# Layer norm at the end of a transformer layer: earlier broadcast, sums on GpSimd, and the last tokens normalised out of PSUM in another order

## The chip, the cores and the metric

The kernel runs on one core of one Trainium2 chip. A core has five engines with a queue each: TensorE (PE: matrix products, written into PSUM), VectorE (DVE), ScalarE (ACT), GpSimd (POOL) and SyncE (SP, which here issues the transfers). The metric is the device time of one execution in microseconds; lower is better. A kernel's time is the median of its runs.

## The reference, cut to what matters

One layer of a diffusion transformer on 1024 tokens of width 1024 (all float32): attention, a layer norm, a SwiGLU feed-forward block with a convolution along the tokens, and a second layer norm. Only the last two lines are touched by the change:

```python
y = _conv_ffn(h, w_up, conv_w, conv_b, w_down)          # silu(gate) * val, then @ w_down
x = _layer_norm(DEEPNORM_ALPHA * x + gate2 * y, ln2_g, ln2_b)

def _layer_norm(x, g, b):
    mu = mean(x); var = mean((x - mu) ** 2)
    return (x - mu) * rsqrt(var + LN_EPS) * g + b
```

## The kernel before

Activations lie transposed: 128 channels of one of eight channel blocks f on the partitions, tokens along the row. Each float32 operand of a product is split into two parts, hi (`hd`, a cast on ScalarE, line 82) and lo (`ld`, a subtraction on VectorE, line 87), and a product of a pair is three matmuls (lines 90 to 92).

The down projection at the end is built from seven products over half the tokens each, p = 1, 6, 2, 7, 4, 5 in a loop, and a seventh, 3, after it. One product has 11 steps k; a step multiplies four channel blocks f with 512 tokens, so four groups of three matmuls. The pair of step k is loaded, cast and split about three steps ahead (`dnext`, `dload`), into rings of four slots, so that the pair of step 10 gets its slot when step 6 has been multiplied. A finished product is added from PSUM into the residual `zz` by VectorE (`accum`, line 1437); these evictions are issued within the next product.

After product 4 the first 512 tokens (`h0`) are complete, and their layer norm runs beside product 5: `ln_steps` (line 1018) makes a list of steps: statistics (tiny matmuls against a column of ones, then a few small operations and a power on GpSimd), diagonals (line 978), the broadcast of 1/sigma and of mean/sigma over the partitions (matmuls at line 1048, copied out by ScalarE at line 1050), and then for each f an apply: a product on VectorE (line 1055), a subtraction (line 1057, with LN2_P = 1 always on GpSimd), and the output with weight and bias on ScalarE (line 1430) with its transfer. Each step carries a gap. `tick` adds columns / 0.8 to a counter after every group of three matmuls and issues the next step when the counter has reached its gap. LN2_D holds the gaps for the first half: before the statistics, the diagonals, the broadcast, the first apply, and each further apply. The steps are queued in step k = 3 of product 5 and the counter starts from zero there.

After product 5 come the casts and splits of the last four pairs of product 3, product 5's evictions (four of its own sums with `modc`, four with `nmod`), then the third quarter (tokens 512 to 767; product 3, tiles `yl`, 256 columns): the first seven steps for all four f, then for each f the last four steps, an `accum`, the sums for the layer norm (`ln_add`: `zs` the sum, line 998, and `zq` the sum of squares, line 999, the squares by ScalarE at line 997), and `tok`, which transposes the block of the last 256 tokens into PSUM tiles `zt` (line 1560). The tiles `zt` of the first call take the banks that product 5's first two blocks have held. The third quarter's layer norm (LN2_E) runs beside the last quarter's product.

The last quarter (two blocks t of 128 tokens) is normalised with tokens on the partitions: `zt[a][t]` holds one half a of the channels, mean and variance come from the batch-norm statistics (lines 1563 and 1597), `bmv` holds mean and then 1/sigma, and four tiles `ot[t, a]` are made, weighted, biased and sent (lines 1602 to 1620).

The order of TensorE's queue is that of the program (the manual schedule opened at line 1177). The queues of the other engines are ordered by the language's planner, which takes the program's order as priority and its own idea of when an instruction is ready; on the chip each queue then runs strictly in that order and waits at each instruction for what it needs.

Of the kernel before, what the change touches and what calls it, by code (L numbers as in the profile page):

```python
# [7 lines left out]
F32 = mybir.dt.float32  # L8
R32 = mybir.dt.float32r
AF = mybir.ActivationFunctionType  # L10
ALU = mybir.AluOpType
AX = mybir.AxisListType

P = 128
# [21 lines left out]
SPAN = 0.8, 0.85  # L36
LN1_F = 3500.0, 5100.0, 100.0
LN1_D = (2500.0, 2000.0, 2000.0, 2500.0), (300.0, 3700.0, 300.0, 500.0), (100.0, 1000.0, 300.0, 500.0)
LN2_D = 5000.0, 4000.0, 2500.0, 1500.0, 700.0
LN2_E = 3500.0, 3000.0, 1500.0, 800.0, 500.0  # L40
NCL = 3
BLD = 2400.0
# [6 lines left out]
D3AT = (7, 5), (7, 9), (4, 1), (4, 4), (4, 7), (4, 10), (5, 2)  # L49
NXS = 5  # L50
RAWB = 3
OTP = (0, 0), (1, 0)
OTO = (0, 0), (0, 1), (1, 0), (1, 1)
OTK = 4
OTA = 1
# [14 lines left out]
def layer_kernel(  # L70
# [6 lines left out]
    nc = tc.nc  # L77
# [55 lines left out]
    def ht(name, shape=(P, T), dt=F32):  # L133
        hslot[name] = pool, tag = hfree.pop(0)
        return pool.tile(list(shape), dt, tag=tag, name=name, bufs=1)
# [94 lines left out]
    for k in range(KT):  # L230
# [5 lines left out]
        for t in range(NT):  # L236
            s = slice(t * P, (t + 1) * P)
# [463 lines left out]
    for n, (gi, k) in enumerate(order):  # L701
# [9 lines left out]
        nm, src, tiles = groups[gi]  # L711
# [4 lines left out]
        for t in tiles:  # L716
            if t < NT:
                s = slice(t * P, (t + 1) * P)
                a = hT[k][0][:, s], hT[k][1][:, s]
            else:  # L720
                s = slice((t - NT) * P, (t - NT + 1) * P)
                a = c[0][:, s], c[1][:, s]
# [164 lines left out]
    def sml(name, w=512):  # L887
        return ps3.tile([P, w], F32, tag="sml", name=name, bufs=2)
# [28 lines left out]
    def zv(f, s):  # L917
        hf = s.start // HALF
        return zt_[f % 4, hf][:, f // 4, s.start - hf * HALF:s.stop - hf * HALF]
# [24 lines left out]
    for f in range(2, KT):  # L944
# [4 lines left out]
        for j in range(4):  # L949
            k = (f % 2) * 4 + j  # L950
            for hf in (0, 1):
                a = O[1, hf, 0, j // 2][:, j % 2], O[1, hf, 1, j // 2][:, j % 2]
# [9 lines left out]
    post = tc.alloc_tile_pool(name="post", bufs=1, side="left", reuse_waits="tile")  # L962
# [26 lines left out]
    def ln_add(zf, zs, zq, s, first, nm, qe, se):  # L989
        w = s.stop - s.start  # L990
        ln_flush()
        if first:
            nc.scalar.activation(zq[:, s], zf, AF.Square)
            nc.gpsimd.tensor_scalar(out=zs[:, s], in0=zf, scalar1=1.0, scalar2=0.0, op0=ALU.mult, op1=ALU.add)
            return
        q = tm(f"sq{nm}", w=w)
        nc.scalar.activation(q, zf, AF.Square)
        se.tensor_tensor(out=zs[:, s], in0=zs[:, s], in1=zf, op=ALU.add)
        sqs.append(lambda: qe.tensor_tensor(out=zq[:, s], in0=zq[:, s], in1=q, op=ALU.add))
# [13 lines left out]
    def drain(keep=0):  # L1013
        while len(pend) > keep:
            pend.pop(0)[1]()
            clock[0] = 0.0
# [170 lines left out]
    for f in (4, 6):  # L1187
        for si in (1, 2):
# [3 lines left out]
            elif f == 6:  # L1192
                second = ln1(2)
                a = [n for n in range(len(pend)) if len(pend) - n <= KT]
# [294 lines left out]
    lnr = ht("lnr", (P, 2, HALF)), ht("lnr2", (P, 2, HALF))  # L1489
# [8 lines left out]

    def sums(f, s, first):
        ln_add(zv(f, s), zs2, zq2, s, first, f"b{f}_{s.start}", nc.vector,  # L1500
               nc.vector if s.start else nc.gpsimd)

    for p in (1, 6, 2, 7, 4, 5):
        if p == 6:
# [10 lines left out]
        def ev(f, o, p=p):  # L1515
            if p == 1:
                nc.scalar.copy(u2[f], o)
            elif p == 6:
                accum(f, h0, u2[f], False)
                nc.vector.tensor_tensor(out=u2[f], in0=u2[f], in1=o, op=ALU.subtract)  # L1520
            elif p == 2:
                accum(f, h0, o, True)
                sums(f, h0, f == 0)
                accum_affine(f, h1, u2[f], True)
            elif p == 7:
                nc.vector.tensor_tensor(out=u3[f], in0=u2[f], in1=o, op=ALU.add)
                accum(f + 4, h0, u3[f], True)
                accum_affine(f + 4, h1, u3[f], False)
                if f == 3:
                    hput("u20", "u21", "u30", "u31")  # L1530
            elif p == 4:
                accum(f + 4, h0, o, True)
                sums(f + 4, h0, False)
            else:
                accum(f + 4, h1, o, False)
                sums(f + 4, LN2_S[1], f == 0)

        evict += [lambda f=f, o=acc[f]: ev(f, o) for f in range(4)]
        if p == 4:
            after.append(lambda: pend.extend(ln_steps(zs2, zq2, h0, "b0", emit2, *LN2_D, LN2_P[0])))  # L1540
    banks[:] = sides[nside[0] % 2] + sides[nside[0] % 2 ^ 1]
# [6 lines left out]
    s = LN2_S[-1]  # L1548
    w = s.stop - s.start
    nt = w // P  # L1550
    zt = {}
    bst = post.tile([P, nt, 2, 6], F32, tag="bst", name="bst")
    mv = post.tile([P, nt, 2], F32, tag="bmv", name="bmv")
    nm = post.tile([P, nt], F32, tag="bnm", name="bnm")

    def tok(f):
        if f % 4 == 0:
# [28 lines left out]
    for f in range(4):  # L1586
        o = sml(f"yl{f}_{r.start}")[:, 0:r.stop - r.start]
# [9 lines left out]
        nc.vector.bn_aggr(out=mv[:, t], in_=bst[:, t].rearrange("p a b -> p (a b)"))  # L1597
    nc.vector.tensor_scalar(out=mv[:, :, 1], in0=mv[:, :, 1], scalar1=LN_EPS, scalar2=None, op0=ALU.add)
    nc.gpsimd.tensor_tensor(out=mv[:, :, 1], in0=mv[:, :, 1], in1=mhalf[:, 0:nt], op=ALU.pow)
    nc.vector.scalar_tensor_tensor(out=nm, in0=mv[:, :, 0], scalar=-1.0, in1=mv[:, :, 1], op0=ALU.mult, op1=ALU.mult)  # L1600
    ot = {}

    def last(t, a):
        o = ot[t, a]
        nc.vector.tensor_tensor(out=o, in0=o, in1=lnr[0][:, a], op=ALU.mult)
        e = nc.gpsimd if (t, a) in OTP else nc.vector
        e.tensor_tensor(out=o, in0=o, in1=lnr[1][:, a], op=ALU.add)
        ts = slice(s.start + t * P, s.start + (t + 1) * P)
        nc.sync.dma_start(out[4 * a:4 * a + 4, :, ts].rearrange("f p q -> p f q"),
                          o.rearrange("p (f q) -> p f q", q=P))  # L1610

    drain(OTK)
    for n in OTO:
        t, a = n
        o = ot[n] = ht(f"ot{t}_{a}", (P, HALF))
        nc.scalar.activation(o, zt[a][t], AF.Identity, bias=nm[:, t:t + 1], scale=mv[:, t, 1:2])
        drain(max(len(pend) - OTA, 0))
    for t, a in OTO:
        last(t, a)
        drain(max(len(pend) - OTB, 0))  # L1620
# [116 lines left out]
```

## Time and profile before

| | |
|---|---|
| median of 3 runs | 1587.97 us (1587.14 to 1588.69) |
| span of the profiled execution, first to last instruction | 1585.4 us |
| around the span, median less span | 2.57 us |
| granted TensorE clock, mean | 0.992 |
| instructions | 22064 |

The profiled execution's own time is known by its span alone; all instants below are microseconds from the span's start. A row of a timeline has the start, the time the instruction (or the merged run, with its count) took, the engine, the line, the operation, what it writes and reads, the shapes, and in brackets the idle time of the engine before it with what ended that. A row of a table of stretches has the busy time of each engine in the stretch, the granted TensorE clock (1.00 is full speed), the share of the DMA engines and the rate. Consecutive instructions of one engine overlap by up to 0.1 us, so that a run of equal ones is shorter than their number times the time of one.

### The profile page before, as it was taken

Reading aid. Unit: us, or ns where it says so; the run is one execution under the profiler, and the core shown is the slowest. Engines: PE = TensorE matmul, PEld = TensorE weight load, DVE = VectorE, ACT = ScalarE, POOL = GpSimd, SP = SyncE. Lnnn points to the kernel's source line nnn. Section 1 sums busy time; section 2 is a strip of 40 time slices with the busy share of each in tenths; the row PEclk is TensorE's granted clock in tenths of the full one; section 3 lists DMA queues with packets and bytes.
Section 4 is the critical chain, followed back from the end, with each engine's and each line's share of the span. In section 5 each row is a group of like instructions: output and inputs, shape, how many; then the busy total and the mean of one; then the engine's idle time right before and its main releaser. Section 6 shows DMA issues by size and latency. Waiting matters only on the chain.

```text
span 1585.4 us, 22064 instructions
## 1 busy us (share of the span) xinstructions
PE 1528.4 (96%) x7680; PEld 1269.8 (80%) x7680; DVE 1195.6 (75%) x1766; ACT 813.0 (51%) x1443; POOL 753.7 (48%) x731
## 2 busy tenths in 40 slices
PE   6999999999999999999999999999999999999996
PEld 5878788878887887777788898888888888888876
DVE  7797646628888777888674779888888877657886
ACT  5422222448887667688531565444444444435642
POOL 0574302426667556665422554666667764021132
PEclk9999999999999999999999999999999999999998
DMA  9695662322236555531451132333334446996721
GB/s 378 217 313 188 221 217 81 120 80 67 62 104 157 139 127 145 118 73 39 142 186 53 60 101 86 114 107 112 115 106 118 111 113 189 358 273 210 255 94 53
DMA packets 112367, 229.98 MB, mean 145 GB/s; under 512 B 12960, under 2 KB 27808, under 8 KB 112160
## 3 DMA queue, kind: packets, MB, share of 16 engines
q1 hardware_dynamic: 96816, 198.93, 37.6%
q0 software_dynamic: 10400, 20.19, 8.2%
q10 hardware_dynamic: 5040, 9.46, 1.6%
q8 instruction: 60, 0.98, 0.3%
q14 instruction: 51, 0.42, 0.1%
HBM read 177.35 MB, written 65.86 MB: 153 GB/s over the span
## 4 chain that ended last, share of the span: by engine, by line
PE 82%; DVE 6%; ACT 4%; issue 3%; POOL 2%; DMA 2%; ACTq 0%; SPq 0%; DVEq 0%; POOLq 0%
PE ptr L531 5%; PE p L90 4%; PE p L91 4%; PE p L92 4%; PE g L90 3%; PE g L91 3%; PE g L92 3%; PE b L92 3%; PE b L91 3%; PE b L90 3%; PE s L414 2%; PE a L92 2%; PE c L91 2%; PE d L91 2%; PE c L92 2%
## 5 line engine op out<-in xcount | busy, mean ns | idle before, releaser
L541 DVE TENSOR_TENSOR ptl<-ptr,pth 128x512 fp32r<-128x512 f32 x188 | 124.8, 685 | 27.5 <-ACT pth L540 25.2
L531 PE MATMUL ptr<-ident,p 128*128 128x128 f32 x816 | 126.5, 278 | 10.3 <-DVE ptl L541 7.8
L540 ACT CAST pth<-ptr 128x512 fp32r<-128x512 f32 x188 | 106.6, 588 | 56.3 <-PE ptr L531 32.7
L87 DVE TENSOR_TENSOR ld<-rd,hd 128x1024 fp32r<-128x1024 f32 x77 | 94.0, 1240 | 52.5 <-ACT hd L82 50.4
L426 ACT ACTIVATE p<-p,nm 128x1024 f32<-128x1024 f32 (+2 forms) x128 | 125.3, 981 | 10.9 <-DVE p L459 10.1
L531 PEld LDWEIGHTS ptr<-ident,p 128*128 128x128 f32 x816 | 93.8, 140 | 40.3 <-DVE ptl L541 13.5
L82 ACT CAST hd<-rd 128x1024 fp32r<-128x1024 f32 x77 | 79.2, 1050 | 81.5 <-PE p L92 50.0
L552 PE MATMUL av<-pth,VT 128*128 128x512 f32 x236 | 104.6, 443 | 1.0 <-ACT avs L558 0.5
L90 PE MATMUL p<-hd 128*128 128x512 f32 x264 | 103.2, 391 | 0.0
L92 PE MATMUL p<-hd,ld 128*128 128x512 f32 x264 | 102.7, 389 | 0.0
L91 PE MATMUL p<-ld,hd 128*128 128x512 f32 x264 | 102.7, 389 | 0.0
L90 PE MATMUL g<-hh,whg 128*128 128x512 f32 x256 | 99.9, 390 | 0.0
L92 PE MATMUL g<-hh,wlg 128*128 128x512 f32 x256 | 99.7, 389 | 0.0
L91 PE MATMUL g<-hl,whg 128*128 128x512 f32 x256 | 99.6, 389 | 0.0
L553 PE MATMUL av<-ptl,VT 128*128 128x512 f32 x236 | 97.6, 414 | 2.0 <-POOL ptl L87 1.9
L87 POOL TENSOR_TENSOR wlg<-wg,whg 128x512 fp32r<-128x512 f32 x32 | 47.0, 1479 | 109.6 <-ACT whg L82 107.3
L459 DVE TENSOR_SCALAR_CACHE_REDUCE p<-s,cvt,nmc 128x1024 f32<-128x1024 f32 x64 | 84.5, 1340 | 12.3 <-PE s L415 11.8
L414 PE MATMUL s<-KL,q 128*128 128x512 f32 (+2 forms) x192 | 76.0, 396 | 2.9 <-ACT p_x L426 2.0
L188 DVE CUSTOM_DVE_ANT_0 wml<-wml,sc,bmc 128x1024 f32<-128x1024 f32 x32 | 45.0, 1416 | 39.0 <-DMA wml<-in_wmodT_dram 38.6
L84 POOL TENSOR_SCALAR pth<-prw 128x512 fp32r<-128x512 f32 x48 | 31.1, 649 | 88.2 <-ACT prw L537 62.7
L82 ACT CAST wS<-s 128x512 fp32r<-128x512 f32 x76 | 45.3, 621 | 52.1 <-POOL s L1079 51.3
L415 PE MATMUL s<-KL,q 128*128 128x512 f32 (+2 forms) x192 | 71.7, 373 | 0.0
(396 smaller groups left out, 4974.0 us busy)
## 6 DMA issues: line engine op xcount, KB each, us to landing
wml<-in_wmodT_dram SPq DMA_DIRECT2D x48, 512.0 KB
ru<-in_w_up_dram SPq DMA_DIRECT2D x38, 512.0 KB
rd<-td SPq DMA_DIRECT2D x55, 256.0 KB
rd<-sd SPq DMA_DIRECT2D x44, 256.0 KB
rd<-in_w_dn_dram SPq DMA_DIRECT2D x33, 256.0 KB
wm<-in_wmodT_dram SPq DMA_DIRECT2D x16, 512.0 KB
wg<-in_w_g_dram SPq DMA_DIRECT2D x32, 256.0 KB
sgd<-sg ACTq DMA_DIRECT2D x32, 256.0 KB
```

The lines of the kernel that those rows point to most:

```text
L82: nc.scalar.copy(hi, src)
L87: lo_eng.tensor_tensor(out=lo, in0=src, in1=hi.bitcast(F32), op=ALU.subtract)
L90: nc.tensor.matmul(ps, a[0], b[0], start=start, stop=False, skip_group_check=resumed)
L91: nc.tensor.matmul(ps, a[0], b[1], start=False, stop=False, skip_group_check=resumed)
L92: nc.tensor.matmul(ps, a[1], b[0], start=False, stop=stop, skip_group_check=resumed)
L414: nc.tensor.matmul(o, self.q[0][:, hs], ks, start=True, stop=False)
L426: nc.scalar.activation(p, s, AF.Exp, bias=nm[:, h:h + 1], scale=scale, accum_out=sm[:, h:h + 1])
L531: nc.tensor.transpose(tr[:, h * P:(h + 1) * P], self.pslice(h, n), ident)
L540: nc.scalar.copy(hi, tr)
L541: nc.vector.tensor_tensor(out=lo, in0=tr, in1=hi.bitcast(F32), op=ALU.subtract)
L552: nc.tensor.matmul(self.av, v, hi, start=first, stop=False)
L553: nc.tensor.matmul(self.av, v, lo, start=False, stop=self.left == 0)
```

## The change

Three edits, all at the end of the kernel:

- LN2_D, the gaps of the first half's layer norm, is changed: shorter gaps before the statistics, the diagonals, the broadcast and the first apply, a longer one between applies.
- The `zs` sums of the third quarter are issued on GpSimd in place of VectorE; the first half's were there already.
- The last tokens: before, ScalarE made (z - mean) / sigma out of PSUM, with the product -mean/sigma (`bnm`) computed ahead of it, VectorE multiplied with the weight, and VectorE or GpSimd (OTP) added the bias. Now VectorE makes (z - mean) * weight out of PSUM in one pass for all four tiles; for the first token block ScalarE then scales with 1/sigma and GpSimd adds the bias, and for the second one VectorE does both in one pass.

```diff
-LN2_D = 5000.0, 4000.0, 2500.0, 1500.0, 700.0
+LN2_D = 4000.0, 2800.0, 2000.0, 1200.0, 1300.0
...
-OTP = (0, 0), (1, 0)
+OTP = (0, 0), (0, 1)
...
     def sums(f, s, first):
         ln_add(zv(f, s), zs2, zq2, s, first, f"b{f}_{s.start}", nc.vector,
-               nc.vector if s.start else nc.gpsimd)
+               nc.gpsimd)
...
-    nm = post.tile([P, nt], F32, tag="bnm", name="bnm")
...
-    nc.vector.scalar_tensor_tensor(out=nm, in0=mv[:, :, 0], scalar=-1.0, in1=mv[:, :, 1], op0=ALU.mult, op1=ALU.mult)
...
     def last(t, a):
         o = ot[t, a]
-        nc.vector.tensor_tensor(out=o, in0=o, in1=lnr[0][:, a], op=ALU.mult)
-        e = nc.gpsimd if (t, a) in OTP else nc.vector
-        e.tensor_tensor(out=o, in0=o, in1=lnr[1][:, a], op=ALU.add)
+        if (t, a) in OTP:
+            nc.scalar.activation(o, o, AF.Identity, scale=mv[:, t, 1:2])
+            nc.gpsimd.tensor_tensor(out=o, in0=o, in1=lnr[1][:, a], op=ALU.add)
+        else:
+            nc.vector.scalar_tensor_tensor(out=o, in0=o, scalar=mv[:, t, 1:2], in1=lnr[1][:, a],
+                                           op0=ALU.mult, op1=ALU.add)
...
         o = ot[n] = ht(f"ot{t}_{a}", (P, HALF))
-        nc.scalar.activation(o, zt[a][t], AF.Identity, bias=nm[:, t:t + 1], scale=mv[:, t, 1:2])
+        nc.vector.scalar_tensor_tensor(out=o, in0=zt[a][t], scalar=mv[:, t, 0:1], in1=lnr[0][:, a],
+                                       op0=ALU.subtract, op1=ALU.mult)
```

## The prediction

> **What bounds the kernel now.** I read the page first, then the stalls of TensorE, then the stretch around its one long stall, then the end. TensorE is the bound nearly everywhere:
>
> ```profile
> PE 1528.4 (96%) x7680; PEld 1269.8 (80%) x7680; DVE 1195.6 (75%) x1766; ACT 813.0 (51%) x1443; POOL 753.7 (48%) x731
> ```
>
> The diff touches only what is issued from 1509 us on, so the waits of TensorE from 1505 us to the end come next. There is one group:
>
> ```profile
> PE zt L1560 <- DVE zz L1437: 4.1, 3, 3.4
> ```
>
> In TensorE's order of time the stall stands between the last matmul of the first column block of the third quarter and the transposes of the last tokens (start, duration, engine, line, tiles, idle before and what ended it):
>
> ```profile
> 1541.75 0.28 PE L92 MATMUL yl<-hd,ld 128*128 128x256 f32 x1
> 1545.47 0.33 PE L1560 MATMUL zt<-ident,zz 128*128 128x128 f32 x1 [3.44 <-DVE zz L1437]
> ...
> 1550.90 0.38 PE L1560 MATMUL zt<-ident,zz 128*128 128x128 f32 x2
> ...
> 1552.55 0.38 PE L1560 MATMUL zt<-ident,zz 128*128 128x128 f32 x2
> ```
>
> Without the stall the first transposes would start at 1541.87 (the matmuls are 0.12 apart) and, at the warm step of 1552.55 - 1550.90 = 1.65 per block, the fourth pair at 1541.87 + 3 x 1.65 = 1546.82. It starts at 1552.55, so this place holds 5.73 us. Part of that is the clock. The busy time and clock of single stretches (busy us of PE, PEld, DVE, ACT, POOL, then PEclk, DMA share, GB/s):
>
> ```profile
> 98.10:100.60 2.50, 0.10 (x2) 0.08 (x1) 2.50 (x4) 1.19 (x2) 2.50 (x2) 0.77 0.71 227
> 716.90:718.60 1.70, 0.14 (x2) 0.12 (x2) 1.67 (x6) 1.11 (x5) 0.47 (x2) 1.00 0.87 217
> 719.00:724.00 5.00, 5.00 (x29) 3.75 (x28) 3.86 (x7) 4.71 (x13) 0.88 (x2) 1.00 0.00 0
> 1542.00:1545.40 3.40, 0.03 (x1) 0.00 (x0) 3.40 (x9) 1.05 (x3) 0.00 (x0) 1.00 0.00 0
> 1546.80:1550.10 3.30, 3.30 (x18) 3.30 (x17) 3.06 (x8) 0.83 (x2) 0.00 (x0) 0.50 0.00 0
> ```
>
> After the stall the granted clock is 0.50 for 3.3 us, which costs half of it, 1.65. A gap of about 2.4 us near 98 us also halves the clock; one of about 1.56 us near 717 us does not, then or after. So a stall left under some 1.6 us should cost only itself.
>
> What the transposes wait for is older than the diff's last part: they are written into the PSUM banks of product 5, whose accumulations into zz VectorE finishes late. VectorE's order:
>
> ```profile
> 1518.99 1.23 DVE L87 TENSOR_TENSOR ld<-rd,hd 128x1024 fp32r<-128x1024 f32 x1 [1.35 <-ACT hd L82]
> 1520.75 11.49 DVE L1055 TENSOR_TENSOR zz<-zz,rbb 128x512 f32<-128x512 f32 x8 [0.54 <-ACT rbb L1050]
> 1532.17 0.74 DVE L1437 SCALAR_TENSOR_TENSOR zz<-p,modc,zz 128x512 f32<-128x512 f32 x1
> 1536.47 4.63 DVE L87 TENSOR_TENSOR ld<-rd,hd 128x1024 fp32r<-128x1024 f32 x4 [3.56 <-ACT hd L82]
> 1541.02 1.40 DVE L1437 SCALAR_TENSOR_TENSOR zz<-p,modc,zz 128x512 f32<-128x512 f32 x2
> 1542.34 0.41 DVE L998 TENSOR_TENSOR zs<-zs,zz 128x256 f32<-128x256 f32 x1
> 1542.67 0.42 DVE L999 TENSOR_TENSOR zq<-zq,sqb 128x256 f32<-128x256 f32 x1
> ...
> 1544.67 2.72 DVE L1437 SCALAR_TENSOR_TENSOR zz<-p,nmod,zz 128x512 f32<-128x512 f32 x4
> ```
>
> It stands idle 3.56 us for ScalarE's casts of the last four down-weight pairs, and those stand behind ScalarE's eight outputs of the first half, which follow GpSimd's eight subtractions one by one:
>
> ```profile
> 1534.69 0.81 ACT L1430 ACTIVATE of<-zz,ln2c 128x512 f32<-128x512 f32 x1 [0.44 <-POOL zz L1057]
> 1535.41 3.89 ACT L82 CAST hd<-rd 128x1024 fp32r<-128x1024 f32 x4
> ```
>
> ```profile
> 1521.66 12.99 POOL L1057 TENSOR_TENSOR zz<-zz,mbb 128x512 f32<-128x512 f32 x8 [7.68 <-ACT mbb L1050]
> ```
>
> So the chain that ends in the stall begins with the broadcast matmuls of the layer norm, a step whose place LN2_D sets: bcrb, 13 us on GpSimd, four casts, four splits, the accumulations.
>
> **The change part by part.**
>
> *Gaps (LN2_D).* The counter grows by 640 after each group of three matmuls of product 5 and the steps are queued at k = 3. Stepping it by hand gives, before: statistics after group 8, diagonals 15, broadcast 18, applies 21 to 28; after: 7, 11, 14 and 16, 18, ... 30. The broadcast moves up by four groups of three matmuls. The step of the matmuls, the two broadcasts, and the second diagonal on VectorE:
>
> ```profile
> 1518.16 0.39 PE L92 MATMUL p<-hd,ld 128*128 128x512 f32 x1
> 1518.39 0.39 PE L90 MATMUL p<-hd 128*128 128x512 f32 x1
> ...
> 1519.08 1.02 PE L1048 MATMUL bcrb<-dgrb,onesf 128*128 128x512 f32 x2
> 1519.93 1.02 PE L1048 MATMUL bcmb<-dgmb,onesf 128*128 128x512 f32 x2
> ...
> 1515.83 0.68 DVE L978 TENSOR_TENSOR dgmb<-ident,mrb 128x512 f32<-128x512 f32 x1
> ```
>
> 12 x 0.227 = 2.72 us earlier, at 1516.36. TensorE does the same work, only in another order: after the broadcasts (0.85 each by their starts) come 14 groups of 0.68, so product 5 still ends at 1519.08 + 1.7 + 9.5 = 1530.3. The diagonals have time: the second ends at 1516.5 today, and would serve a second broadcast at 1517.2 even if it did not move with the statistics. What is lost: the split of product 5's last pair (the row at 1518.99) now falls among the applies. Its ring slot is freed when TensorE's step k = 6 ends, two groups before the broadcast of before (1517.7), and the broadcasts' 1.7 us now lie inside that step (1519.4). TensorE needs that split four groups before the end of product 5, at 1527.6, so the split has 8 us for a cast of 1 and its own 1.2 to 2.3. But the applies are limited by VectorE and GpSimd excluding each other:
>
> ```profile
> L1055 DVE TENSOR_TENSOR zz<-zz,rbb x8: 687/1776/1781, 1520.8 to 1530.5; 128x512 f32<-128x512 f32 x8
> ...
> 1499.80 2.31 DVE L87 TENSOR_TENSOR ld<-rd,hd 128x1024 fp32r<-128x1024 f32 x1
> ...
> 1497.18 3.85 POOL L998 TENSOR_TENSOR zs<-zs,zz 128x512 f32<-128x512 f32 x2 [48.17 <-DVE zz L1437]
> 1498.09 0.74 DVE L1437 SCALAR_TENSOR_TENSOR zz<-p,nmod,zz 128x512 f32<-128x512 f32 x1
> ```
>
> An apply takes 0.69 alone and 1.78 beside a subtraction, a split 2.31 in place of 1.23; an accumulation with one operand in PSUM keeps its 0.74. So the split adds its own step, 4.63 / 4 = 1.16, to the chain of 13 us. The eight outputs, and with them the four casts and splits, come 2.72 - 1.16 = 1.56 earlier. Ends: 2.7 if the split slips in free, 0.9 if the first accumulation is now put behind the splits (0.66 more on the path). The new "each" of 1300 does nothing by itself: the chain's 1.7 per apply is slower than two groups of matmuls, 1.36.
>
> *Sums of the third quarter on GpSimd.* Seven zs adds leave VectorE; three of them stand ahead of the accumulation that TensorE waits for, at 0.33 each (1542.34 to 1542.67): 1.0 us off the path. On GpSimd, idle there, one takes about
>
> ```profile
> 1564.80 0.79 POOL L1057 TENSOR_TENSOR zz<-zz,mbb 128x256 f32<-128x256 f32 x1 [5.75 <-DVE zz L1055]
> ```
>
> 0.8 us, at most one every 0.7 us ahead of the stall, and the queue empties before the statistics matmuls, which LN2_E puts eleven groups of 3 x 0.12 us, 4 us, after the last block. Against it: two zq adds stay on VectorE in the same stretch, both operands in SBUF, and can be held up by a GpSimd add, as the applies are, by up to 0.5 each. Gain 0.0 to 1.0; I take 0.6, nearer to the upper end since only part of a 0.79 add excludes.
>
> [...]
>
> *Sum at the stall.* 1.56 + 0.6 = 2.2 us earlier, so TensorE idles about 1.3 of 3.44 us. That is under 1.6, so the slow clock goes too: 2.2 + 1.65 = 3.8. Ends: 0.9 (0.9 + 0.0, clock still halved) and 5.73 (stall gone). From there to 1571 us TensorE has no other wait, so the gain is carried to the tail whole. Next late would be the same accumulation, or the statistics of the third quarter: the last block's accumulation, zs add (0.8) and zq add (0.4) have those 4 us.
>
> *The tail.* Rows of before:
>
> ```profile
> 1573.44 0.17 DVE L1598 TENSOR_SCALAR bmv<-bmv 128x2 f32<-128x2 f32 x1
> 1573.69 0.70 POOL L1599 TENSOR_TENSOR bmv<-bmv,mhalf 128x2 f32<-128x2 f32 x1 [3.46 <-DVE bmv L1598]
> 1574.76 2.78 ACT L1616 ACTIVATE ot<-zt,bnm,bmv 128x512 f32<-128x512 f32 x4 [3.39 <-DVE bnm L1600]
> 1576.39 1.66 POOL L1607 TENSOR_TENSOR ot<-ot,lnr 128x512 f32<-128x512 f32 x1 [2.00 <-DVE ot L1605]
> 1579.12 1.74 DVE L1605 TENSOR_TENSOR ot<-ot,lnr 128x512 f32<-128x512 f32 x1
> ...
> 1580.34 0.94 SPq L1609 DMA_DIRECT2D out_dram<-ot  x2
> ...
> 1581.62 0.37 SPq L1609 DMA_DIRECT2D out_dram<-ot  x1
> ...
> 1581.30:1584.00 2.70, 0.00 (x0) 0.00 (x0) 0.29 (x1) 0.00 (x0) 0.00 (x0) 0.50 1.03 284
> ```
>
> Removed: the product bnm (0.16, on the path), four ScalarE passes, four VectorE products, two VectorE adds. Added: four VectorE passes out of PSUM, which need the mean alone and so start at 1573.6 beside GpSimd's power (2.72 for four, the row at 1544.67: to 1576.4); two ScalarE scalings (0.81 each, as the output at 1534.69, from 1574.5), two GpSimd adds behind them (1.66 each: 1575.3 to 1577.0 to 1578.6), and two VectorE passes for the last token block, both operands in SBUF, beside those adds (up to 1.74 each: 1576.4 to about 1579.5). The last output is issued at about 1579.5 in place of 1581.62: 2.1 us. But the outputs queue: the last three (256 KB each, the first issued at 1580.34) fill 2.7 us at 284 GB/s. If the second add's output is issued ahead of the last two, these three start from 1578.65 in place of 1580.34, 1.7; if the order lets one go earlier, up to 2.5. Ends 1.6 and 2.5; I take 2.0, the middle.
>
> *Sum.* 3.8 + 2.0 = 5.8 us off the profiled 1585.4, so a span of 1579.6. The median of the runs is 2.57 above this span, which I take for what lies around it: 1587.97 - 5.8 = 1582.2.
>
> **The rivals.**
>
> (a) *Only the tail gains.* The planner orders ScalarE and VectorE anew, and the four casts or the accumulations come as late as now; the stall stays. For it: the casts could run from 1522 on, and the planner put them behind all eight outputs. Against it: those outputs come earlier in any order. 1587.97 - 2.0 = 1586.0.
>
> (b) *The stall closes.* If the planner fills VectorE's 3.56 us of idle time with accumulations: 5.7 + 2.0 = 7.7, 1580.3.
>
> (c) *The stall shrinks, the clock still falls*, because the remaining gap is 2 us or more: 1.2 + 2.0 = 3.2, about 1584.8. [...]
>
> (d) *Slower: TensorE starves in product 5.* The first three outputs of the half are now issued ahead of product 5's last pair. If ScalarE's queue has that pair's cast behind them, it waits for GpSimd, 1.70 per output. The last output ends at 1535.5 today and so at 1532.8, the one of place j (0 to 7) at 1532.8 - 1.7 x (7 - j), and the split 2.2 (0.97 + 1.23) later; TensorE needs it at 1527.6. Up to j = 2 (1526.5) that costs nothing; with all eight ahead (1535.0) it is 7.4 us of stall and 1.65 to 3.3 of half clock. The old stall would be gone (5.7) and the tail gains 2.0: +1.4 to +3.0, about 1590.2. Below seven outputs in front it is a smaller gain, not a loss. Against it: the cast is ready before the second output, and today no cast of product 5 waits behind an output.
>
> **How the numbers follow.** Forecast 0.60, (b) 0.12, (c) 0.08, (a) 0.12, (d) 0.08. A difference of 0.2%, 3.2 us, is about what a measurement of this kernel can tell from none. Faster by more: forecast (less 0.02 for the low ends of both its terms), (b) and half of (c): 0.74. Within: (a), the rest of (c) and 0.02 of the forecast: 0.18. Slower: (d), which lies about at that bound and is counted there whole, since a second late split would add 2.7: 0.08. The range goes from 1579.6 (5.73 + 2.5 = 8.2) to 1586.4 (tail alone at its low end, 1.6) and leaves out (d) and some of the rest.
>
> **What would show it.** Broadcast matmuls at about 1516.4; eight subtractions of 1.7 from about 1519 with one longer step; the four casts starting near 1533.9; the wait of zt on zz at 1 to 1.5 us, with the clock at 1.00 after it; L998 on POOL with 0.8 us each; at the end L1616's line on VectorE with four steps of 0.68, and 1.7 to 2.5 us less from the last statistic to the last output. It is wrong if TensorE waits within product 5, if the stall stays above 2 us, or if the tail's two VectorE passes wait for both GpSimd adds and the output queue eats the rest.

## The result and the profile after

| | before | after |
|---|---|---|
| median of the runs | 1588.39 us (14 runs, 1587.14 to 1590.55) | 1585.94 us (14 runs, 1583.75 to 1589.05) |
| ratio to before | | 0.9985, 95% interval 0.9978 to 0.9992 |
| span of the profiled execution | 1585.4 us | 1582.0 us |

The changed kernel is 2.45 us faster where 5.8 was forecast. That is a small difference, 0.15% and less than the 0.2% that the prediction took for the least that a measurement tells from none, but the interval leaves out no change. The median lies within the forecast's range of 1579.6 to 1586.4 us.

The wait that the forecast looked at is gone, and there is a new one. The waits of TensorE in the changed kernel from 1485 us on (engine, line, tile, releaser: us in all, times, longest):

```profile
PE p L91 <- DVE ld L87: 3.7, 1, 3.7
PE zt L1559 <- DVE zz L1437: 0.4, 1, 0.4
```

The 0.4 belongs to the very last block, where before had the same 0.36. So the 3.44 us of `zt` have closed to nothing, and product 5 (tiles `p`), which ran without a gap before, now stands still for 3.72 us within its last four groups of three matmuls. TensorE's timeline of the changed kernel: a matmul four places ahead of product 5's first, the stall, the first matmul of the third quarter, and the fourth pair of transposes:

```profile
1493.09 0.39 PE L92 MATMUL p<-hd,ld 128*128 128x512 f32 x1
...
1524.81 0.39 PE L90 MATMUL p<-hd 128*128 128x512 f32 x1
1528.93 0.80 PE L91 MATMUL p<-ld,hd 128*128 128x512 f32 x1 [3.72 <-DVE ld L87]
...
1533.78 0.42 PE L90 MATMUL yl<-hd 128*128 128x256 f32 x1
...
1550.69 0.38 PE L1559 MATMUL zt<-ident,zz 128*128 128x128 f32 x2
```

What TensorE waited for is on VectorE, whose timeline of the changed kernel reads:

```profile
1513.45 1.22 DVE L87 TENSOR_TENSOR ld<-rd,hd 128x1024 fp32r<-128x1024 f32 x1 [0.45 <-ACT hd L82]
1515.20 11.46 DVE L1055 TENSOR_TENSOR zz<-zz,rbb 128x512 f32<-128x512 f32 x8 [0.53 <-ACT rbb L1050]
1526.59 2.28 DVE L87 TENSOR_TENSOR ld<-rd,hd 128x1024 fp32r<-128x1024 f32 x1
1531.82 3.50 DVE L87 TENSOR_TENSOR ld<-rd,hd 128x1024 fp32r<-128x1024 f32 x3 [2.94 <-ACT hd L82]
1535.23 1.40 DVE L1437 SCALAR_TENSOR_TENSOR zz<-p,modc,zz 128x512 f32<-128x512 f32 x2
```

The row at 1526.59 is the split of product 5's last pair. Before, it stood ahead of the eight applies; now all eight stand ahead of it, 11.46 us, and it takes 2.28 in place of 1.23, beside GpSimd's last subtractions (1.22 in e11_after_lock below, where GpSimd has none). Its cast is not what is late. ScalarE's timeline of the changed kernel:

```profile
1521.08 0.82 ACT L1430 ACTIVATE of<-zz,ln2c 128x512 f32<-128x512 f32 x1 [0.88 <-POOL zz L1057]
1521.80 1.04 ACT L82 CAST hd<-rd 128x1024 fp32r<-128x1024 f32 x1
...
1530.04 0.81 ACT L1430 ACTIVATE of<-zz,ln2c 128x512 f32<-128x512 f32 x1 [1.40 <-POOL zz L1057]
1530.76 2.92 ACT L82 CAST hd<-rd 128x1024 fp32r<-128x1024 f32 x3
```

The cast stood behind three outputs and was done at 1522.84, 2.4 us before TensorE ran dry at 1525.20; the split then waited 3.75 us in VectorE's queue.

The clock paid as well. Stretches of the changed kernel, in the columns explained with the profile before:

```profile
1524.49:1527.90 3.41, 0.71 (x4) 0.25 (x2) 3.41 (x3) 1.70 (x3) 3.41 (x3) 1.00 0.42 156
1527.90:1531.31 3.41, 2.38 (x6) 1.92 (x7) 0.97 (x1) 2.01 (x3) 2.10 (x1) 0.50 0.41 150
1531.31:1534.72 3.41, 3.41 (x12) 2.85 (x11) 2.90 (x3) 3.06 (x4) 0.00 (x0) 0.50 0.21 77
```

Two steps of 3.41 us at half clock, where before had one (its row, 1546.80 to 1550.10, is in the prediction). In them the matmuls of product 5 start 0.42 us apart (1529.52 to 1529.94) in place of 0.23, so a step costs about half of TensorE's busy time in it: an estimated 1.2 and 1.7 us here.

At the end of the program, the parts that the forecast spoke of (VectorE, GpSimd and ScalarE of the changed kernel):

```profile
1571.22 0.33 DVE L1596 BATCH_NORM_AGGREGATE bmv<-bst 128x2 f32<-128x12 f32 x2
1571.52 0.75 DVE L1617 SCALAR_TENSOR_TENSOR ot<-zt,bmv,lnr 128x512 f32<-128x512 f32 x1
1572.19 0.16 DVE L1597 TENSOR_SCALAR bmv<-bmv 128x2 f32<-128x2 f32 x1
1572.26 2.06 DVE L1617 SCALAR_TENSOR_TENSOR ot<-zt,bmv,lnr 128x512 f32<-128x512 f32 x3
1572.42 0.70 POOL L1598 TENSOR_TENSOR bmv<-bmv,mhalf 128x2 f32<-128x2 f32 x1 [4.04 <-DVE bmv L1597]
1573.15 1.34 ACT L1604 ACTIVATE ot<-ot,bmv 128x512 f32<-128x512 f32 x2 [3.65 <-POOL bmv L1598]
1573.95 2.93 POOL L1605 TENSOR_TENSOR ot<-ot,lnr 128x512 f32<-128x512 f32 x2 [0.83 <-ACT ot L1604]
1574.23 3.21 DVE L1607 SCALAR_TENSOR_TENSOR ot<-ot,bmv,lnr 128x512 f32<-128x512 f32 x2
```

The new passes are as cheap as forecast (four in 2.8 us, 0.74 each). But the first of them slipped in ahead of the addition of epsilon (1572.19), and GpSimd's power, ScalarE's scalings and the last passes on VectorE wait for that one.

**How the places are compared.** The start of product 5, taken here and in the expectations as the matmul four places (0.9 us) ahead of its first, lies at 1495.91 in the profile of before and at 1493.09 in that of after, though nothing that was changed runs ahead of it, and between 1493.1 and 1500.5 over all profiles here. So spans can't be compared to a microsecond: of the 3.4 us between the two spans above, 2.8 lie ahead of product 5. From there on the profiles agree with each other to some hundredths wherever they do the same work, and the table takes them apart: A from this start to the fourth pair of transposes `zt`, B from there to the last transpose, C from the last transpose to the end of the span. "Stall" is TensorE's longest wait in A, "half clock" the stretch at 0.50 that begins in A. These columns are of one profiled execution each; the ratio is of the timed runs.

| kernel | A | B | C | sum | stall in A | half clock | ratio to before |
|---|---|---|---|---|---|---|---|
| before | 56.64 | 19.12 | 13.74 | 89.49 | 3.44 (zt) | 3.41 | |
| after | 57.61 | 19.12 | 12.16 | 88.89 | 3.72 (p) | 6.83 | 0.9985 [0.9978, 0.9992] |
| e1_gaps | 57.55 | 19.12 | 13.74 | 90.41 | 3.73 (p) | 6.83 | 0.9996 [0.9987, 1.0005] |
| e2_sums | 55.81 | 19.12 | 13.73 | 88.65 | 2.60 (zt) | 3.41 | 0.9992 [0.9982, 1.0002] |
| e3_tail | 57.27 | 19.12 | 12.17 | 88.56 | 3.44 (zt) | 6.83 | 0.9992 [0.9982, 1.0002] |
| e4_ahead | 54.58 | 19.12 | 12.16 | 85.86 | 1.36 (zt) | 3.41 | 0.9976 [0.9964, 0.9989] |
| e6_split | 55.13 | 19.11 | 12.17 | 86.41 | 2.15 (zt) | 3.41 | 0.9976 [0.9965, 0.9986] |
| e7_evict | 51.05 | 20.17 | 12.16 | 83.38 | none | none | 0.9963 [0.9951, 0.9976] |
| e8_evict_before | 52.13 | 20.91 | 13.71 | 86.76 | 0.99 (zt) | none | 0.9993 [0.9984, 1.0002] |
| e9_lock | 50.92 | 19.12 | 13.72 | 83.76 | none | none | 0.9960 [0.9947, 0.9972] |
| e10_lock_tail | 50.93 | 19.12 | 12.18 | 82.23 | none | none | 0.9950 [0.9937, 0.9964] |
| e11_after_lock | 50.92 | 19.12 | 12.18 | 82.22 | none | none | 0.9944 [0.9931, 0.9956] |
| e12_eps | 50.92 | 19.12 | 11.58 | 81.62 | none | none | 0.9942 [0.9930, 0.9954] |

A without stall and at full clock is 50.92. Before lost 5.72 us there (5.73 in the prediction), after loses 6.69: in these two executions the change swapped one stall for another at a loss of 0.97 and won 1.58 in C.

### The profile page after: what moved, and what is told of

Same layout as the page of the kernel before. It is cut to its first block, busy times and chain, and to the rows that moved or that the text cites. A ratio compares the mean times of both kernels' runs of the same rounds, so it can differ in the third digit from the quotient of the medians.

```text
span 1582.0 us, 22065 instructions
## 1 busy us (share of the span) xinstructions
PE 1526.0 (96%) x7680; PEld 1266.0 (80%) x7680; DVE 1192.4 (75%) x1758; ACT 811.3 (51%) x1441; POOL 759.6 (48%) x738
## 4 chain that ended last, share of the span: by engine, by line
PE 79%; DVE 9%; ACT 4%; DMA 4%; issue 3%; POOL 2%; SPq 0%; DVEq 0%; ACTq 0%; POOLq 0%
PE ptr L531 5%; PE p L91 4%; PE p L92 4%; PE p L90 4%; PE b L92 3%; PE b L91 3%; PE b L90 3%; PE a L91 2%; PE d L91 2%; PE c L91 2%; PE d L90 2%; PE c L90 2%; PE a L90 2%; PE c L92 2%; PE d L92 2%
## 5 line engine op out<-in xcount | busy, mean ns | idle before, releaser
L87 POOL TENSOR_TENSOR wlg<-wg,whg 128x512 fp32r<-128x512 f32 x32 | 43.3, 1362 | 112.7 <-ACT whg L82 112.7
```

What stands on the lines that cost most here:

```text
L87: lo_eng.tensor_tensor(out=lo, in0=src, in1=hi.bitcast(F32), op=ALU.subtract)
```

## The experiments

Two theories were set against each other. Q, the queue: the gain of the shorter gaps was lost because the split of product 5's last pair stands behind eight applies on VectorE. S: the gaps won what was forecast, and the sums and the tail fell short.

**The three edits one by one.** e1_gaps is the kernel before with the new LN2_D alone:

```diff
-LN2_D = 5000.0, 4000.0, 2500.0, 1500.0, 700.0
+LN2_D = 4000.0, 2800.0, 2000.0, 1200.0, 1300.0
```

> The kernel before with the new gaps alone. Theory Q (the queue): the split of product 5's last pair stands behind all eight applies on VectorE, so TensorE stalls in product 5 for 3.5 to 4 us and then runs 3.4 to 6.8 us at half clock (1.7 to 3.4 lost), while the stall before the last tokens' transposes falls from 3.44 to under 1.5 us and its half clock goes (4 to 5.7 gained): 0 to +3 us against before. Rival S (the gaps gain what was forecast, and the sums or the tail fell short): -3 to -4 us, with no stall in product 5.

e2_sums has the `zs` sums of the third quarter on GpSimd alone:

```diff
         ln_add(zv(f, s), zs2, zq2, s, first, f"b{f}_{s.start}", nc.vector,
-               nc.vector if s.start else nc.gpsimd)
+               nc.gpsimd)
```

> The kernel before with the third quarter's zs sums on GpSimd alone. Q: the stall before the transposes shrinks by 0 to 1.0 us and stays above 2.4, the half clock stays, so -1.0 to 0 us. S: the sums cost time, +0.5 or more, since the zq adds beside them are held up.

e3_tail has the tail alone (the hunks of the diff on OTP, `nm`, `last` and the four passes).

> The kernel before with the last tokens' new passes alone. Both theories: from the last transposes to the end 13.9 us become 12.2 to 12.4, so -1.5 to -2.0 us. S allows less: -0.5 or nothing over the runs.

e1 has the stall in product 5 and both steps of half clock, and the stall of `zt` gone, so the gaps alone make the whole of after's A (57.55 against 57.61): 0.92 us more than before. TensorE's waits in e1_gaps, and then in e2_sums:

```profile
PE p L91 <- DVE ld L87: 3.7, 1, 3.7
PE zt L1560 <- DVE zz L1437: 0.4, 1, 0.4
```

```profile
PE zt L1560 <- DVE zz L1437: 3.3, 3, 2.6
```

e2 takes 0.84 off the stall of `zt` (3.44 to 2.60), a little more than the 0.6 forecast, and all of it arrives in the sum. But it lies at the stall that the new gaps close in their own way, so in the changed kernel it has nothing left to shorten. e3 wins 1.57 in C and leaves the stall at 3.44; that its A is 0.63 longer is the clock, which fell for two steps there and for one in before, at the same stall. S falls with e1, which has none of the sums and the tail: it has the stall in product 5 that S denied, and the 3 to 4 us less that S expected (ratio 0.9975 to 0.9981) lie outside its interval. The timed intervals of e1 to e3 each include no change, so what the parts are worth rests on the profiles.

**The order on VectorE and ScalarE.** e4_ahead is the changed kernel with the cast of product 5's last pair queued ahead of the outputs and its split ahead of the fourth and later applies; the last two gaps were put so that the program's order follows. (`behind(a, b, fn)` issues a step with its instructions queued behind the instructions a and b.)

```diff
-LN2_D = 4000.0, 2800.0, 2000.0, 1200.0, 1300.0
+LN2_D = 4000.0, 2800.0, 2000.0, 4600.0, 700.0
...
-        split(r, h, l, nc.scalar, nc.vector)
+        if (p, k) == (5, NH - 1):
+            last5[:] = [nc.scalar.copy(h, r).ins,
+                        nc.vector.tensor_tensor(out=l, in0=r, in1=h.bitcast(F32), op=ALU.subtract).ins]
+        else:
+            split(r, h, l, nc.scalar, nc.vector)
...
+                for n, (gap, fn) in enumerate(steps[3:]):
+                    pend.append((gap, lambda n=n, fn=fn: behind(last5[0], last5[n >= 3], fn)))
```

> The changed kernel, with the cast of product 5's last pair queued ahead of all outputs on ScalarE and its split ahead of the fourth apply on VectorE (gaps 4000, 2800, 2000, 4600, 700, so that the applies are issued after that pair). Q: no stall in product 5 and no half clock there; the stall before the transposes comes back at 0.5 to 1.6 us without the half clock; 4 to 6 us less than the changed kernel, 0.995 to 0.996 of before. S: the stall in product 5 has another cause and stays; within 1 us of the changed kernel.

No stall in product 5, 3.03 us less than after in A, ratio 0.9976. The split still runs beside GpSimd (2.31), but in time. The gain is short of the 4 to 6 us that were expected, since the stall of `zt` that came back, 1.36 us as expected, has a step of half clock behind it. The stretches of e4_ahead:

```profile
1538.49:1541.90 3.41, 1.73 (x13) 1.33 (x12) 3.41 (x7) 0.84 (x2) 1.97 (x3) 1.00 0.00 0
1541.90:1545.31 3.41, 3.41 (x18) 3.41 (x18) 2.77 (x6) 0.42 (x2) 0.73 (x1) 0.50 0.00 0
```

e4 moves two queues at once. e6_split keeps the new gaps and ScalarE's order and moves only VectorE's: in the diff above the last line becomes

```diff
+                    pend.append((gap, lambda n=n, fn=fn: behind(last5[1], last5[1], fn) if n >= 3 else fn()))
```

> The changed kernel with its new gaps, and one order more: the fourth to eighth apply of the first half's layer norm are queued on VectorE behind the split of product 5's last pair; its cast stays where it is, behind three outputs on ScalarE. VectorE theory (the split came too late because eight applies, 1515.20 to 1526.67, stood ahead of it): the cast ends near 1522.8, the split by 1525.2, and the stall of TensorE in product 5 goes from 3.72 us to 0 to 0.5; the applies left over end some 2 us later than in the changed kernel, so the stall of the transposes before the last product is back at 1 to 3 us; from the start of product 5 to the end of the program 86 to 88 us instead of 88.9, ratio to the kernel before 0.996 to 0.998. ScalarE theory (the forecast's own rival: the cast behind the outputs is what holds TensorE): the split still ends after 1527, product 5 still stalls for 2 us or more, and the time stays with the changed kernel's, 0.9985.

The cast again stands behind three outputs. ScalarE and VectorE of e6_split:

```profile
1525.88 0.81 ACT L1435 ACTIVATE of<-zz,ln2c 128x512 f32<-128x512 f32 x1 [0.44 <-POOL zz L1057]
1526.61 1.04 ACT L1226 CAST hd<-rd 128x1024 fp32r<-128x1024 f32 x1
```

```profile
1520.45 2.99 DVE L1055 TENSOR_TENSOR zz<-zz,rbb 128x512 f32<-128x512 f32 x3
1527.67 1.23 DVE L1227 TENSOR_TENSOR ld<-rd,hd 128x1024 fp32r<-128x1024 f32 x1 [4.23 <-ACT hd L1226]
1528.82 6.39 DVE L1055 TENSOR_TENSOR zz<-zz,rbb 128x512 f32<-128x512 f32 x5
```

From product 5's start (1498.34 here) the cast starts after 28.3 us, in the changed kernel after 28.7; with the cast in the same place, product 5 has no stall. So it was VectorE's queue and not ScalarE's that held TensorE. VectorE now idles 4.23 us ahead of the split, the applies end later, and the stall of `zt` is back at 2.15.

**The banks of product 5.** Two kernels put product 5's evictions in pairs, so that the first two blocks' banks come free earlier: e7_evict on top of e4_ahead, e8_evict_before alone on top of the kernel before.

```diff
-    for e in evict:
-        e()
     for f in range(4):
+        evict[f]()
         accum(f, h1, acc[f], True)
```

> The kernel of e4_ahead, and beside it the PSUM evictions of product 5 put in pairs block by block, so that the banks of its first two blocks come free earlier. Theory that the wait left over before the last product (1.36 + 0.33 us, and one step of half clock) is one for these banks: the stall closes to under 0.5 us, no step of half clock is left near the end, and from the start of product 5 to the end of the program 82 to 83 us instead of 85.9; ratio to the kernel before 0.993 to 0.995. Rival: the accumulations behind the evictions are bound by VectorE's total work in that stretch, so another order of the same work only moves the wait to a later transpose: 85 to 86 us, ratio 0.9965 to 0.9985.

> The kernel before with that one edit, evictions of product 5 in pairs block by block, and none of the change. Theory of the banks: the stall of 3.44 + 0.33 us shrinks to 1 to 1.5, one step of half clock stays (as it did after 1.36 us in e4_ahead): 2 to 2.5 us less, ratio 0.9983 to 0.9988. If the stall under 1.6 us costs no half clock, as the forecast assumed, 4 us less: ratio 0.9975. Rival (VectorE's total work binds): within 0.5 us of the kernel before, ratio 0.9997 to 1.0003.

The stall closes in e7 and shrinks to 0.99 in e8, both without half clock, so it was a wait for those banks. (The step of half clock that was expected of e8 did not come. The gain in the sums is 2.73 us, where 2 to 2.5 was expected with that step and 4 without.) But 1.05 (e7) and 1.79 (e8) us of it come back in B, where the third quarter's sums are later. The waits of e8_evict_before:

```profile
PE zt L1559 <- DVE zz L1437: 1.4, 2, 1.0
PE stb L1031 <- DVE zs L998: 0.8, 1, 0.8
PE stb L1032 <- DVE zq L999: 0.5, 1, 0.5
```

That is the rival of e7's expectation in part: some of the wait only moves, and e7 ends at 83.38 where 82 to 83 was expected. In the sums e7 gains 2.48 on e4 and e8 2.73 on before; the timed ratios show less of it than was expected (e7 0.9963 for 0.993 to 0.995; e8 0.9993, upper end of the gain 0.16%, 2.5 us), which stays open.

**VectorE beside GpSimd.** e9_lock is the kernel before with the subtractions of the mean of the first half on VectorE: eight more instructions there, eight fewer on GpSimd.

```diff
-LN2_P = 1, 2, 2
+LN2_P = 9, 2, 2
```

> The kernel before with the first half's eight subtractions of the mean taken from GpSimd to VectorE (all nine steps there), and none of the change. It measures what VectorE and GpSimd lose side by side in this stretch: in the kernel before the eight applies take 13.6 us from first to last, beside GpSimd's. Theory that they hold each other up: an apply alone takes 0.7 us instead of 1.7, so subtraction and apply together cost VectorE no more than the apply alone did beside GpSimd, the chain ends 2 to 4 us earlier, the stall before the last product falls under 1.5 us: 2 to 5 us less in all, ratio 0.997 to 0.9988. Rival (each engine works at its own speed, VectorE only gets 5.5 us of work more): the stall grows by 1 to 5 us, ratio 1.0005 to 1.003.

The rows of line 1055 and 1057 of e9_lock (times of one: least, median, greatest in ns; first and last start):

```profile
L1055 DVE TENSOR_TENSOR zz<-zz,rbb x8: 680/684/694, 1520.1 to 1528.0; 128x512 f32<-128x512 f32 x8
L1057 DVE TENSOR_TENSOR zz<-zz,mbb x8: 679/683/686, 1521.3 to 1529.2; 128x512 f32<-128x512 f32 x8
```

and of line 1057 of the kernel before:

```profile
L1057 POOL TENSOR_TENSOR zz<-zz,mbb x8: 1298/1740/1744, 1521.7 to 1533.4; 128x512 f32<-128x512 f32 x8
```

VectorE does all sixteen in 9.8 us, less than the 11.5 that the eight applies alone took beside GpSimd. From the first apply to the last subtraction it is 9.8 us in place of 13.9 (1520.75 to 1534.65), the casts no longer hold VectorE up, and both stall and half clock go: A is at the 50.92 of no stall and full clock, a gain of 5.72 us from one number. Expected were 2 to 5, with a ratio of 0.997 to 0.9988; measured is 0.9960.

**The better kernels.** e10_lock_tail is e9_lock with the change's tail. e11_after_lock is the whole changed kernel with LN2_P = 9, 2, 2. e12_eps is e10_lock_tail with the four passes out of PSUM queued behind the addition of epsilon:

```diff
-    nc.vector.tensor_scalar(out=mv[:, :, 1], in0=mv[:, :, 1], scalar1=LN_EPS, scalar2=None, op0=ALU.add)
+    eps = nc.vector.tensor_scalar(out=mv[:, :, 1], in0=mv[:, :, 1], scalar1=LN_EPS, scalar2=None, op0=ALU.add).ins
...
-        nc.vector.scalar_tensor_tensor(out=o, in0=zt[a][t], scalar=mv[:, t, 0:1], in1=lnr[0][:, a],
-                                       op0=ALU.subtract, op1=ALU.mult)
+        with tc.issue_after(eps):
+            nc.vector.scalar_tensor_tensor(out=o, in0=zt[a][t], scalar=mv[:, t, 0:1], in1=lnr[0][:, a],
+                                           op0=ALU.subtract, op1=ALU.mult)
```

> The kernel of e9_lock (gaps and sums of the kernel before, the first half's subtractions on VectorE) with the change's tail. Theory that the two gains lie one behind the other: from the start of product 5 to the end of the program 83.8 us of e9_lock less the tail's 1.55, so 82.2; ratio to the kernel before 0.994 to 0.996. Rival: part of e9_lock's gain was a profile that ran well, and the ratio stays at 0.996 to 0.998.

> The changed kernel whole, its new gaps too, with one edit: the first half's subtractions of the mean on VectorE. The split of product 5's last pair then stands behind three applies and two subtractions instead of eight applies. Queue theory: these five end some 3.5 us after the first starts, product 5 has no stall, the eight steps end some 10.5 us after they began, the transposes have no stall, no step of half clock falls before the tail: 82 to 82.5 us from the start of product 5 to the end, ratio 0.994 to 0.996. Rival (shorter gaps cost TensorE its product 5 wherever the subtractions run, since the chain's work then falls into product 5): 2 us or more of stall in product 5 and one or two steps of half clock, 85 to 89 us, ratio 0.997 to 0.9985.

> The kernel of e10_lock_tail with the four passes out of PSUM queued behind the small instruction that adds epsilon; in the changed kernel the first pass (0.74 us) stood ahead of it and put off GpSimd's power, on which ScalarE's scalings and VectorE's last passes wait. Theory that the chain of epsilon, power, scaling and add sets the end: 0.6 to 0.7 us less than e10_lock_tail, 81.5 us from the start of product 5 to the end. Rival: VectorE's own row of passes or the four output transfers set the end, and the time stays within 0.2 us of e10_lock_tail.

e10 and e11 come out alike, 82.2 us: with the subtractions on VectorE the change's gaps neither cost nor gain, since its split now stands behind three applies and two subtractions. VectorE of e11_after_lock:

```profile
1522.56 1.29 DVE L1055 TENSOR_TENSOR zz<-zz,rbb 128x512 f32<-128x512 f32 x2 [0.53 <-ACT rbb L1050]
1523.78 1.29 DVE L1057 TENSOR_TENSOR zz<-zz,mbb 128x512 f32<-128x512 f32 x2
1524.98 0.69 DVE L1055 TENSOR_TENSOR zz<-zz,rbb 128x512 f32<-128x512 f32 x1
1525.59 1.22 DVE L87 TENSOR_TENSOR ld<-rd,hd 128x1024 fp32r<-128x1024 f32 x1
```

e12 takes another 0.60 off C, as expected of the chain from epsilon on. Both e11 (1580.36 us, beside 1589.09 of before) and e12 (1580.45) beat before and after; their intervals overlap.

## What the prediction had right and wrong, point by point

- *The number*: forecast 1582.2, measured 1585.94, a gain of 2.45 for 5.8. It lies in the range because the slow end of the range was the tail's gain alone, and the tail is the part that came out. The forecast's larger part, 3.8 us at the stall, did not. That the median lies beside the 1586.0 of rival (a) is luck: there the old stall stays, here it closed and another took its place. By the sign that the prediction gave itself, "It is wrong if TensorE waits within product 5", its account is wrong.
- *The broadcast 2.72 earlier*: right. ScalarE copies it out 24.22 us after product 5's start before (1520.13) and 21.49 after (1514.58), 2.73 less.
- *Outputs and casts 1.56 earlier*: near in size, 1.83 (the first of the four casts from 39.50 to 37.67 after product 5's start). Of the 2.73 the chain gave up 0.90 and not 1.16, since the split ran beside the last subtractions and not among the applies (GpSimd's eight take 13.89 us in place of 12.99).
- *The split of product 5's last pair "falls among the applies"*, and "has 8 us for a cast of 1 and its own 1.2 to 2.3": this step failed. The 8 us were counted from when its data can be there to when TensorE needs it, and the split was taken to slip in among the applies; in VectorE's queue all eight, 11.46 us, stand ahead of it. It ended 3.7 us too late, and with the half clock that follows A holds 0.97 us more than before in place of 3.8 less. A miss of 4.8 us.
- Rival (d) named this very stall, but on ScalarE's queue. Its own count was right there ("Up to j = 2 (1526.5) that costs nothing": the cast stood behind three outputs and was 2.4 us early). It was not made for VectorE's queue, though there the applies start as soon as the broadcast is copied out, and the eight hold the queue for 11.46 us.
- *The wait of `zt`*: it vanished, but not by the forecast's sum: TensorE came to it some 6 us later, held up in product 5.
- *Sums 0.6*: 0.84 by itself (e2); no gain in the changed kernel, where the stall that it would shorten is gone. What spoke against it, a `zq` sum held up by a GpSimd sum, cost 0.2 per case (0.60 against 0.41 us in e11_after_lock), part of a GpSimd sum's 0.79 as the 0.6 assumed, and not the up to 0.5 feared.
- *The tail 2.0*: 1.58, just under the low end of 1.6 to 2.5. The forecast had the four passes start beside GpSimd's power; the one that slipped ahead of epsilon put the power off and cost 0.60 (e12). Without it C gains 2.16.
- *A stall under 1.6 us costs no half clock*: not safe as it stands. 0.99 cost none (e8), but 1.36 with 0.33 close behind cost one step (e4). What went with the half clock here, but for one place, is a short busy time of TensorE in the 3.41 us ahead of it, and not the single gap alone: near 98 us, from where the prediction drew its gap of 2.4 us, before has 1.35 us of work from 96.05 to 99.46 and then half clock, and e9_lock has 1.67 from 97.76 to 101.17 and then full clock (last section).
- The sum: 3.8 + 2.0 forecast; -0.97 + 1.58 = 0.6 in the two profiles, 2.45 in the medians, with 1.3 to 3.5 in the interval. Where the steps of half clock fell can explain the difference but is not shown to. At the same stall as before, e3_tail lost a second step and 0.63 us more, and with one step in place of two A of after would be 1.2 us shorter (an estimate: half of the 2.38 busy us of the first); the two together would turn the 0.6 into 2.4. e1_gaps has the same difference: 0.92 us slower in its profile, 1.22 faster in the medians beside it (1587.12 against 1588.34; 0.6 by its ratio). A timed run has only the mean clock of the whole execution, which one step moves by 0.001, so it can't tell where a step fell.

## What to carry to other kernels

When an edit lets a chain start earlier, list, for each queue that the chain runs through, what the engine that sets the time still needs from that queue, and count the chain's own instructions ahead of it; here ScalarE's queue was counted and VectorE's was not. Where two engines slow each other side by side, as VectorE and GpSimd do here (an apply took 1.78 us in place of 0.69), try all the work on the faster one before arranging its start: here sixteen instructions on VectorE took 9.8 us, less than the 11.5 of eight beside GpSimd, and that one number was worth more than the whole change. And compare profiles from a common event near the change, since the stretch ahead of it differed by up to 7 us between executions here.

## What the runs showed of the hardware

**Half clock came in stretches of 3.41 or 6.83 us, most of them after little work on TensorE.** That is the length of every stretch at half clock in the table, and of every one that ends within the traces of before and after. A step here is a stretch of 3.41 us, cut where a half clock begins; for e8_evict_before and e9_lock, which keep full speed below, the place of the cut is an estimate. Beside the steps shown of after and e4_ahead, here are those of e8_evict_before, of e3_tail and, from a far earlier place, of e9_lock, each step followed by the next:

```profile
1539.38:1542.79 3.41, 2.42 (x21) 2.23 (x20) 3.41 (x6) 0.42 (x1) 0.00 (x0) 1.00 0.00 0
1542.79:1546.20 3.41, 3.41 (x32) 3.41 (x31) 3.41 (x8) 0.84 (x2) 0.00 (x0) 1.00 0.00 0
```

```profile
1542.09:1545.50 3.41, 1.25 (x11) 1.04 (x9) 3.41 (x8) 0.84 (x3) 0.00 (x0) 0.99 0.00 0
1545.50:1548.91 3.41, 1.94 (x8) 1.65 (x9) 3.41 (x7) 0.41 (x1) 0.00 (x0) 0.50 0.00 0
1548.91:1552.32 3.41, 3.41 (x18) 3.41 (x17) 2.70 (x7) 0.83 (x2) 0.00 (x0) 0.51 0.00 0
```

```profile
97.76:101.17 3.41, 1.67 (x7) 1.41 (x8) 3.41 (x6) 0.62 (x1) 3.32 (x3) 1.00 0.88 309
101.17:104.58 3.41, 3.41 (x16) 2.83 (x16) 3.41 (x8) 0.62 (x1) 2.63 (x2) 1.00 0.87 270
```

TensorE busy for 2.42 (e8) and 1.67 of 3.41 us (e9) kept full speed; 1.73 (e4) and 1.25 (e3) cost the next step half of it. These busy times give no bound, since one of 1.67 kept what one of 1.73 lost. The step ahead of each stretch at half clock had 1.35 (to 99.46 us), 0.90 (to 1546.70) and 0.97 busy us (to 1574.02) in before, and 0.71 (to 1527.90) and 0.84 (to 1572.30) in after, but for one place: near 870 us the clock fell in before after a step with 3.24 busy us. This step and the next read:

```profile
867.47:870.88 3.41, 3.24 (x23) 2.67 (x21) 1.71 (x2) 0.00 (x0) 1.26 (x1) 1.00 0.00 0
870.88:874.29 3.41, 3.41 (x10) 2.74 (x10) 1.85 (x6) 0.00 (x0) 1.03 (x1) 0.50 0.00 0
```

The first holds sixteen statistics matmuls of a single column (128 x 1), listed with 0.25 us each on average; why the clock fell there is not shown. Half clock went on after steps with 1.94 (e3) and 2.38 busy us (after), and ended after steps with 3.41. The stall of 3.44 us cost one step in before, with 0.90 us of work in the step ahead and 3.41 in the slow one, and two in e3, with 1.25 and 1.94. That the place of the stall against the steps decides this is a reading of these two profiles, and no run shows it by itself.

**A pair that gets slower by running side by side.** An apply and a subtraction of 128 x 512 take 1.70 us per pair side by side on VectorE and GpSimd, and 1.21 one after the other on VectorE. On GpSimd the last subtraction, with no apply beside it, took 1.30 (the least in the row of the kernel before), so the pair overlaps in part, where the prediction has the two engines excluding each other: 0.61 (the step of an apply alone) and 1.30 are 1.91. In e9_lock, with no subtraction on GpSimd, an apply takes 0.68, where in the kernel before the median is 1.78.
